# Two Strassen pairs in the output projection, and the third head's attention by float32r parts

## The chip, the core and the metric

The kernel runs on one core of a Trainium2 chip. The core has five engines that run side by side and wait for each other by semaphores: TensorE (PE, matmuls into the PSUM accumulators), VectorE (DVE), ScalarE (ACT), GpSimd (POOL) and SyncE (SP, which issues transfers; ACT issues some too). The metric is the device time of one execution in microseconds (us).

## The reference

One decoder layer on 512 tokens of width 1024, all in float32. It is the chain below; the middle line of the output projection and the two lines of the head are what the change touches.

```python
u    = rms_norm(x, mix_pre_g) * (1 + sc1) + sh1      # sh1, sc1, g1, sh2, sc2, g2 = split(silu(c) @ ada_w + ada_b)
qk_raw, v, o_pre, gates, glu = split(u @ w_in)
q, k = split(silu(causal_dwconv(qk_raw, 4 taps)))    # four heads of 256
# per head, chunks of 128 tokens:
scores = einsum("bhtd,bhsd->bhts", q, k) * exp(dmat - m)
num    = w_inter * (q @ C) + einsum("bhts,bhse->bhte", scores, v)
h    = rms_norm(num / den, ml_norm_g) * sigmoid(o_pre)
y    = silu(layer_norm(causal_dwconv(a * sigmoid(gt), 31 taps)))
mix  = concatenate([h, y]) @ w_out                   # 512 x 2048 times 2048 x 1024
x    = x + g1 * rms_norm(mix, mix_post_g)
f    = ConvFFN(rms_norm(x, ffn_pre_g) * (1 + sc2) + sh2)
x    = x + g2 * rms_norm(f, ffn_post_g)
```

## The kernel before

Most products of two float32 matrices are done in three float32r matmuls (`mm3`, L186). Each operand is split into a high part, a float32r copy that ACT makes, and a low part, the difference; the products high x high, high x low and low x high are accumulated. For weights `w_split` (L164) lets ACT make the high copy and POOL the low part; for activations `pair` (L451) lets DVE make the low part. Names end in h and l for the parts: `wo_0h`, `hl`, `yh`.

**Heads.** The loop over h does the attention of head h (`attention`, L500) while `head_proj` projects q, k and the output gate of head h + 1; `make_v` projects its values. `attention` is a generator whose steps are interleaved with the projections. Scores `s` of one key chunk go through DVE into `E` (the decay weights), and `o` is the product of E and v. `SPLIT` names the heads whose scores and values are done by parts; it is the fourth alone (`SPLIT = (H - 1,)`). The other heads use plain float32 matmuls (L514, L533). ACT copies o into `hn`, POOL works out its norm `fac`, DVE scales hn, PE turns it (`hT`), and DVE and ACT make the gated rows `hh`, `hl`. The taps of q and k (`conv4`) are three shifted multiply-adds on DVE into `q_0c`, `q_1c`, `k_2c`, `k_3c`, read from the projection's PSUM bank `qko`, and then a Silu on ACT.

**Output projection.** The 2048 rows of w_out are 16 blocks of 128: 0 to 7 belong to the heads (two each), 8 to 15 to the convolution. `MIX` gives their order. The left half of the columns is accumulated in the four banks `mixa`, one for 128 tokens, over all 16 blocks (`mix_first`, 12 matmuls of 512 columns for each block), while the attention of the fourth head is done in between. The right half, `mixb`, is done for the first 8 blocks block by block, and for the last 8 token tile by token tile (`mix_last`), because the norm and the feed-forward of the first tile start as soon as it is finished.

**Conditioning.** `mod`, 48 columns, is silu(c) times ada_w, done on DVE in 48 blocks (`ada_block`, L147): a load of 512 KB on ACT's queue and one 128 x 1024 multiply-accumulate with the output `junk`. Blocks 16 to 23 stand behind the convolution's last tap, 24 to 39 behind the fourth head's last low part (`last_lo`); `spare` is memory that the projection's input u leaves free. The gains made from them are turned by PE (`gT`) and sent through memory to become rows (`g1r`, `gs2r`, `sh2r`).

A scheduler sets the order on each engine from dependences and priorities. `in_order()` (L70) pins what is written inside it to the written order on DVE, ACT and POOL.

Of the kernel before, what the change touches and what calls it, by code (L numbers as in the profile page):

```python
# [22 lines left out]
H = 4  # L23
# [25 lines left out]
MIX = [*range(6), *range(8, 14), 6, 7, 14, 15]  # L49
# [3 lines left out]
def decoder_layer(ctx, tc, w_glu0, x, xT, c, adaT, vecs, w_glu, w_qko, w_v0, w_v, w_out, w_up, w_down, out):  # L53
# [93 lines left out]
    def ada_block(i, behind):  # L147

        if i % 6 < 4 and 24 <= i < 40:
            r = spare[0][:, 2 * (i % 6) : 2 * (i % 6) + 2, :].rearrange("p j t -> p (j t)")  # L150
        else:
            r = adas.tile([P, D], F32, tag="ada", name=f"ada_{i}")
        nc.scalar.dma_start(r, adaT[i // 2][:, (i % 2) * D : (i % 2 + 1) * D])
        junk = small.tile([P, D], BF16, tag="junk", bufs=1, name=f"junk_{i}")
        t = V.scalar_tensor_tensor(out=junk, in0=r, scalar=1.0, in1=cb, op0=ALU.mult, op1=ALU.mult, accum_out=mod[:, i : i + 1])  # L155
        tc.add_manual_dep(t.ins, behind.ins.name, mybir.DependencyInfo(mybir.DependencyClass.NoSync, mybir.DependencyReason.DATA),
                          reason="order on VectorE")
# [6 lines left out]
    def w_split(src, name, pool=None, tag="w", eng=None):  # L164
# [6 lines left out]
        (eng or G).tensor_tensor(out=lo[:, :n], in0=src, in1=hi[:, :n].bitcast(F32), op=ALU.subtract)  # L171
        return hi, lo

    def w_load(view, name, pool=None, tag="w"):

        n = view.shape[1]
        r = raws.tile([P, 2048], F32, tag="raw", name=name)
        nc.sync.dma_start(r[:, :n], view)
        return [w_split(r[:, a : min(a + T, n)], f"{name}_{a}", pool, tag) for a in range(0, n, T)]
# [6 lines left out]
    def mm3(ps, a, b, start, stop):  # L186

        PE.matmul(ps, a[0], b[0], start=start, stop=False)  # L188
        PE.matmul(ps, a[0], b[1], start=False, stop=False)  # L189
        PE.matmul(ps, a[1], b[0], start=False, stop=stop)  # L190
# [221 lines left out]
    SPLIT = (H - 1,)  # L412
# [38 lines left out]
    def pair(z, hi, lo):  # L451
        S.activation(hi, z, AF.Copy)
        V.tensor_tensor(out=lo, in0=z, in1=hi.bitcast(F32), op=ALU.subtract)
        return hi, lo

    def conv4(ps, i, name):
# [6 lines left out]
        S.activation(t, t, AF.Silu)  # L463
# [7 lines left out]
    last_conv4 = [None]  # L471
# [9 lines left out]
    def head_proj(h, i):  # L481
# [9 lines left out]
        else:  # L491
            t = slot(f"so{h}_{i}")
            S.activation(t, ps, AF.Tanh, scale=0.5)
            so.append(t)
        if (h, i) in CV_BEHIND:
            cv_block(CV_BEHIND[h, i], last_conv4[0])

    last_lo = [None]

    def attention(h):  # L500
# [46 lines left out]
        for tt in range(NT):  # L547
            hv = hn[tt // 2][:, (tt % 2) * DH : (tt % 2 + 1) * DH]
            V.tensor_scalar(out=hv, in0=hv, scalar1=fac[:, tt : tt + 1], scalar2=None, op0=ALU.mult)
        yield  # L550
        for e in range(2):
# [4 lines left out]
            t = so[e]  # L556
            V.scalar_tensor_tensor(out=t, in0=t, scalar=1.0, in1=tp, op0=ALU.add, op1=ALU.mult)
            hi, lo = slot(f"hh{h}_{e}", F32R), slot(f"hl{h}_{e}", F32R)
            g = ghalf[:, 2 * h + e : 2 * h + e + 1]
            S.activation(hi, t, AF.Copy, scale=g)  # L560
            last_lo[0] = V.scalar_tensor_tensor(out=lo, in0=t, scalar=g, in1=hi.bitcast(F32), op0=ALU.mult, op1=ALU.subtract)
            hy[2 * h + e] = (hi, lo)
# [87 lines left out]
    def send_rows(a, n, queue=nc.scalar):  # L650

        ps = mmbank(f"gT{a}") if a == KT else atbank(f"gT{a}")
        PE.transpose(ps[:n, :P], gains[:, a : a + n], ident)
        t = slot(f"gTs{a}")[:, :P]
        V.tensor_copy(t[:n, :], ps[:n, :P])
        for i in range(n // KT):
# [34 lines left out]
    KA = 8  # L691
# [4 lines left out]
    def wo_rows(hf, g):  # L696
        return w_load(w_out[hf, g], f"wo{hf}_{g}")
# [74 lines left out]
    def norm_rows():  # L772
        yb = rms_bcast(yr[0], T, 1.0 / D, "ry", cvbank)
        for j in range(KT):
            V.tensor_tensor(out=ys[j], in0=ys[j], in1=yb, op=ALU.mult)
            S.activation(ys[j], ys[j], AF.Silu, bias=vcol("cv_ln_b", j), scale=vcol("cv_ln_g", j))
            hi, lo = slot(f"yh{j}", F32R), slot(f"yl{j}", F32R)
# [4 lines left out]
    for h in range(H - 1):  # L782
# [50 lines left out]
    next(steps)  # L833
    for n in range(7, 10):
        mix_first(n)
    for _ in steps:
        pass
    spare.append(upool.tile([P, KT, T], F32, tag="ul", name="spare"))
    for i in range(24, 40):
        ada_block(i, last_lo[0])  # L840
    ada_done(24, 40)
    for n in range(10, 2 * KT):
        mix_first(n)
        if n == 10:
            send_rows(0, KT)
    mg = [slot(f"mg{tt}") for tt in range(NT)]
    x1 = [[slot(f"x1_{tt}_{hf}") for hf in range(2)] for tt in range(NT)]
    wide1 = vpool.tile([P, 2 * T + 8], F32, tag="vh", name="g1r")
    g1r = row(0, lambda n: [wide1[:, :T], wide1[:, T : 2 * T]], "g1")
    for tt in range(NT):  # L850
        for hf in range(2):
            nc.scalar.dma_start(x1[tt][hf], x[tok(tt), hf * T : (hf + 1) * T])
    for tt, ps in enumerate(mixa):
        V.tensor_tensor(out=mg[tt], in0=ps, in1=g1r[0], op=ALU.mult)
        sq_sum(ps, msq[:, 2 * tt : 2 * tt + 1], f"mixa{tt}")
    banks = [atbank(f"mixb{tt}") if tt < 2 else cvbank(f"mixb{tt}") for tt in range(NT)]
    for n_, k in enumerate(MIX[:KA]):
        if n_ % 4 == 0:
            wo = wo_rows(1, n_ // 4)
        for tt, ps in enumerate(banks):  # L860
            mm3(ps, (hy[k][0][:, tok(tt)], hy[k][1][:, tok(tt)]), wo[n_ % 4], n_ == 0, False)
    V.scalar_tensor_tensor(out=gains[:, KT : 2 * KT], in0=sc2[:, :, 0], scalar=1.0, in1=vcols("ffn_pre_g", 0, KT), op0=ALU.add, op1=ALU.mult)
    V.tensor_scalar(out=gains[:, KT : 2 * KT], in0=gains[:, KT : 2 * KT], scalar1=RD, scalar2=None, op0=ALU.mult)
    V.tensor_copy(gains[:, 2 * KT : 3 * KT], sc2[:, :, 1])
    wo = [w for g in range(KA // 4, 4) for w in wo_rows(1, g)]

    HT = T // 2
# [69 lines left out]
    up_w = {0: w_load(w_up[0], "wup0", slots, "t")}  # L937
    raw1 = raw_up(1)
    send_rows(KT, 2 * KT, nc.sync)
    gs2r = row(1, cvtile, "gs2", nc.sync)  # L940
    sh2r = row(2, cvtile, "sh2", nc.sync)
    raw2 = raw_up(2)
    early += [[mmbank(f"up{i}_{half}") for half in range(2)] for i in range(2)]
    with in_order():
        for tt in range(3):
            mix_last(tt, 0, 2 * KT - KA)
        up_split(1, raw1, slots, "t")
        r = chain_sums(0)
# [11 lines left out]
        mix_last(3, 7, 2 * KT - KA)  # L960
# [310 lines left out]
def _layout(i):  # L1271
# [9 lines left out]
    def tiles(w, starts, per):  # L1281
# [21 lines left out]
    wo = f("w_out")[0]  # L1303
    return {
# [10 lines left out]
        "w_out": c_(wo.reshape(2 * KT, P, 2, T)[MIX].reshape(4, NT, P, 2, T).transpose(3, 0, 2, 1, 4).reshape(2, 4, P, 4 * T)),  # L1315
# [22 lines left out]
```

## Time and profile before

| | |
|---|---|
| runs | 774.28, 771.67, 771.31 us (median 771.67) |
| profiled execution | 773.07 us, span 771.4 us, granted clock 0.997 |
| busy in the span | PE 758.4, DVE 610.1, ACT 403.8, POOL 352.2 us |
| third head's attention | about 261 to 300 us of the span |
| output projection, left half | from 320.4 us |
| gT8 turned | 392.7 us |

Times in the trace are us from the span's start. A row of the timeline gives start, duration, engine, line, operation, output and inputs (buffer numbers left out), shape, and how many instructions were merged in it; a bracket at its end is the idle time of the engine before it and what ended it. Neighbouring matmuls overlap, so their cost is taken from start to start. A row of the groups gives the busy time and, behind the comma, the mean in ns of one.

### The profile page before, as it was taken

Reading aid. Unit: us, or ns where it says so; the run is one execution under the profiler, and the core shown is the slowest. Engines: PE = TensorE matmul, PEld = TensorE weight load, DVE = VectorE, ACT = ScalarE, POOL = GpSimd, SP = SyncE. Lnnn points to the kernel's source line nnn. Section 1 sums busy time; section 2 is a strip of 40 time slices with the busy share of each in tenths; the row PEclk is TensorE's granted clock in tenths of the full one; section 3 lists DMA queues with packets and bytes.
Section 4 is the critical chain, followed back from the end, with each engine's and each line's share of the span. In section 5 each row is a group of like instructions: output and inputs, shape, how many; then the busy total and the mean of one; then the engine's idle time right before and its main releaser. Section 6 shows DMA issues by size and latency. Waiting matters only on the chain.

```text
span 771.4 us, 10631 instructions
## 1 busy us (share of the span) xinstructions
PE 758.4 (98%) x3709; PEld 637.5 (83%) x3709; DVE 610.1 (79%) x967; ACT 403.8 (52%) x761; POOL 352.2 (46%) x286
## 2 busy tenths in 40 slices
PE   7999999999999999999999999999999999999996
PEld 5788898778888888988888998888888888888885
DVE  6997999999999966756768798666556687799995
ACT  5447266776666447582253555444444444455762
POOL 2029578696798645443661456444444440000001
PEclk9999999999999999999999999999999999999998
DMA  8983214214022452434953753332233321777872
GB/s 320 377 301 132 90 55 164 82 40 151 30 84 107 153 179 105 164 110 164 366 199 126 253 197 130 130 130 88 110 117 129 130 89 62 255 271 241 298 260 109
DMA packets 36409, 125.33 MB, mean 162 GB/s; under 512 B 4194, under 2 KB 5634, under 8 KB 30468
## 3 DMA queue, kind: packets, MB, share of 16 engines
q1 hardware_dynamic: 24372, 96.17, 35.5%
q10 hardware_dynamic: 11984, 28.48, 10.6%
q8 instruction: 29, 0.48, 0.3%
q14 instruction: 24, 0.20, 0.1%
HBM read 113.22 MB, written 11.42 MB: 162 GB/s over the span
## 4 chain that ended last, share of the span: by engine, by line
PE 72%; DVE 21%; DMA 2%; ACT 2%; issue 2%; POOL 0%; ACTq 0%; DVEq 0%; POOLq 0%
PE up L189 10%; PE up L188 10%; DVE cv L731 10%; PE up L190 10%; PE p L1185 4%; PE glu L189 3%; PE glu L190 3%; PE glu L188 3%; PE p L189 3%; PE p L188 3%; PE p L190 3%; PE mixa L188 2%; PE mixa L190 2%; PE mixa L189 2%; PE mixb L189 2%; PE mixb L188 2%
## 5 line engine op out<-in xcount | busy, mean ns | idle before, releaser
L731 DVE SCALAR_TENSOR_TENSOR cv<-gt,cvw,cv 128x505 f32<-128x505 f32 (+24 forms) x200 | 137.3, 729 | 2.3 <-ACT cv L719 1.1
L685 POOL TENSOR_TENSOR ro2r<-ro2t,mhalf 128x1 f32<-128x1 f32 x1 | 0.5, 537 | 119.8 <-DVE ro2t L683 119.8
L727 POOL TENSOR_TENSOR cs<-cs,cs 128x510 f32<-128x510 f32 (+3 forms) x32 | 41.9, 1308 | 0.3
L171 POOL TENSOR_TENSOR wup_1024l<-wup,wup_1024h 128x512 fp32r<-128x512 f32 x20 | 27.4, 1372 | 31.6 <-ACT wup_1024h L170 31.6
L171 POOL TENSOR_TENSOR wup_0l<-wup,wup_0h 128x512 fp32r<-128x512 f32 x20 | 27.7, 1387 | 30.0 <-ACT wup_0h L170 30.0
L171 POOL TENSOR_TENSOR wup_1536l<-wup,wup_1536h 128x512 fp32r<-128x512 f32 x20 | 28.0, 1399 | 27.6 <-ACT wup_1536h L170 25.1
L155 DVE SCALAR_TENSOR_TENSOR junk<-ada,cb 128x1024 bf16<-128x1024 f32 x20 | 31.3, 1565 | 8.5 <-DMA ada<-in_adaT 8.4
L189 PE MATMUL up<-u2l,wup_0h 128*128 128x512 f32 (+1 forms) x100 | 36.5, 365 | 0.2 <-DVE u2l L910 0.2
L188 PE MATMUL up<-u2h,wup_0h 128*128 128x512 f32 (+1 forms) x100 | 36.5, 365 | 0.0
L188 PE MATMUL up<-u2h,wup_1024h 128*128 128x512 f32 (+1 forms) x100 | 36.4, 364 | 0.0
L190 PE MATMUL up<-u2h,wup_0l 128*128 128x512 f32 (+1 forms) x100 | 36.4, 364 | 0.0
L188 PE MATMUL up<-u2h,wup_512h 128*128 128x512 f32 (+1 forms) x100 | 36.4, 364 | 0.0
L189 PE MATMUL up<-u2l,wup_512h 128*128 128x512 f32 (+1 forms) x100 | 36.4, 364 | 0.0
L190 PE MATMUL up<-u2h,wup_512l 128*128 128x512 f32 (+1 forms) x100 | 36.4, 364 | 0.0
L188 PE MATMUL up<-u2h,wup_1536h 128*128 128x512 f32 (+1 forms) x100 | 36.4, 364 | 0.0
L189 PE MATMUL up<-u2l,wup_1536h 128*128 128x512 f32 (+1 forms) x100 | 36.4, 364 | 0.0
L190 PE MATMUL up<-u2h,wup_1536l 128*128 128x512 f32 (+1 forms) x100 | 36.4, 364 | 0.0
L190 PE MATMUL up<-u2h,wup_1024l 128*128 128x512 f32 (+1 forms) x100 | 36.4, 364 | 0.0
L189 PE MATMUL up<-u2l,wup_1024h 128*128 128x512 f32 (+1 forms) x100 | 36.3, 363 | 0.0
L171 POOL TENSOR_TENSOR wup_512l<-wup,wup_512h 128x512 fp32r<-128x512 f32 x20 | 27.7, 1383 | 14.0 <-ACT wup_512h L170 14.0
L725 ACT ACTIVATE cs<-gt,cvw 128x511 f32<-128x511 f32 (+4 forms) x40 | 27.4, 716 | 6.5 <-POOL cs L727 3.2
L170 ACT ACTIVATE wup_1024h<-wup 128x512 fp32r<-128x512 f32 x22 | 13.9, 631 | 25.1 <-PE up L189 20.4
(1072 smaller groups left out, 2667.0 us busy)
## 6 DMA issues: line engine op xcount, KB each, us to landing
wup<-in_w_up SPq DMA_DIRECT2D x22, 1024.0 KB, 6.5
wqko<-in_w_qko SPq DMA_DIRECT2D x12, 1024.0 KB, 4.8
ada<-in_adaT ACTq DMA_DIRECT2D x20, 512.0 KB, 4.6
ada<-in_adaT SPq DMA_DIRECT2D x16, 512.0 KB, 6.9
wo<-in_w_out SPq DMA_DIRECT2D x8, 1024.0 KB, 4.8
spare<-in_adaT ACTq DMA_DIRECT2D x12, 512.0 KB, 7.4
wd<-in_w_down SPq DMA_DIRECT2D x6, 768.0 KB, 6.7
g2kept<-g2d SPq DMA_DIRECT2D x11, 384.0 KB, 7.3
```

The source lines that it names most:

```text
L155: t = V.scalar_tensor_tensor(out=junk, in0=r, scalar=1.0, in1=cb, op0=ALU.mult, op1=ALU.mult, accum_out=mod[:, i : i + 1])
L170: S.activation(hi[:, :n], src, AF.Copy)
L171: (eng or G).tensor_tensor(out=lo[:, :n], in0=src, in1=hi[:, :n].bitcast(F32), op=ALU.subtract)
L188: PE.matmul(ps, a[0], b[0], start=start, stop=False)
L189: PE.matmul(ps, a[0], b[1], start=False, stop=False)
L190: PE.matmul(ps, a[1], b[0], start=False, stop=stop)
L685: G.tensor_tensor(out=r, in0=t, in1=mhalf[:, :1], op=ALU.pow)
L725: S.activation(t[:, d:], cvx[j][:, : T - d], AF.Copy, scale=w(CK - 1 - d))
L727: G.tensor_tensor(out=side[:, d:], in0=side[:, d:], in1=t[:, d:], op=ALU.add)
L731: last_tap[0] = V.scalar_tensor_tensor(out=cp[:, d:], in0=cvx[j][:, : T - d], scalar=w(CK - 1 - d), in1=cp[:, d:], op0=ALU.mult, op1=ALU.add)
L1185: PE.matmul(ps[q], x, y, start=False, stop=m == NM - 1 and i == 2, skip_group_check=True)
```

## The change

**Strassen pairs.** Conv blocks 12 to 15 leave `MIX`, which has 12 blocks now, and become `PAIRS` (12, 13) and (14, 15). For each pair, the two halves of the tokens, the two blocks of rows and the two halves of the columns make a product of 2 x 2 blocks, done with seven products (Winograd's form) in place of eight. One product (`block`) is two pairs x two token tiles x three parts = 12 matmuls of 512 columns. The order p1, p5, row blocks 10 and 11 of mixa, p2, p6, p4, p7, p3 is written out in one `in_order()` section. The sums of tokens (`token_sums`), of weight rows (`row_sums`, `row_last`, `ot1`), the low parts of both (`token_part`, `row_part`) and the additions between PSUM banks are on DVE; ACT makes the high parts and copies the intermediate products out (`op1`, `op5`, `ou`, `op7`). The raw weight rows (`w_os`, two loads of 1 MB into `wraw`) use memory that u leaves free. The additions are done in place: p5 and p3 in the banks mixb 0 and 1, p1, p6 and p7 in mixb 2 and 3, p2 in mixa 0 and 1, p4 in mixa 2 and 3. After the products mixb gets 4 blocks block by block (`KA = 4`, before 8) and 8 in `mix_last`.

**Third head.** `SPLIT` is now `(H - 2, H - 1)`.

**What moves with it.** Ada blocks 24 to 28 go into the third head's attention, behind taps of the fourth head's q and k; 29 to 34 ahead of hn of the fourth head; 35 to 39 into the written order. The row of g1 and the loads of x go from ACT's queue to SP's. The fourth head's gates (`gate`) are split off so that they can stand in the written order. gT8, `gs2r` and `sh2r` stand inside `mix_last(0)`, behind 5 of its 8 blocks. `wo1_8` and `wup0` are loaded into wraw.

```diff
-MIX = [*range(6), *range(8, 14), 6, 7, 14, 15]
+MIX = [*range(6), *range(8, 12), 6, 7]
+PAIRS = [(12, 13), (14, 15)]
...
-    SPLIT = (H - 1,)
+    SPLIT = (H - 2, H - 1)
...
-    KA = 8
+    HT = T // 2
+    KF = 12
+    KA = 4
...
+    def token_sums(za, zb, name):
+        sums, s4 = cvtile(f"os{name}"), cvtile(f"o4{name}")
+        s1, s2 = sums[:, :HT], sums[:, HT:]
+        V.tensor_tensor(out=s1, in0=za[:, HT:], in1=zb[:, HT:], op=ALU.add)
+        V.tensor_tensor(out=za[:, HT:], in0=za[:, :HT], in1=za[:, HT:], op=ALU.subtract)
+        V.tensor_tensor(out=s2, in0=s1, in1=za[:, :HT], op=ALU.subtract)
+        V.tensor_tensor(out=s4[:, :HT], in0=zb[:, :HT], in1=s2, op=ALU.subtract)
...
+    def row_part(which, m):
+        b = {"p1": 1, "p2": 0, "p6": 1, "p7": 2, "p3": 3, "p4": 0}.get(which)
+        z = ot1[m] if which == "p5" else wraw[m][:, b * T : (b + 1) * T]
+        wf[which, m] = w_split(z, f"o{which}_{m}", eng=V)
...
+    def block(which, m):
+        ps = {"p1": banks[2:], "p6": banks[2:], "p7": banks[2:], "p5": banks[:2], "p3": banks[:2], "p2": mixa[:2], "p4": mixa[2:]}[which]
+        for q in range(2):
+            mm3(ps[q], tf[m][which][q], wf[which, m], m == 0 and which in ("p1", "p5"), m == 1, True)
...
         if h == H - 2:
             norm_mean()
+            tc.cur_priority += LATER
+            for i in range(16, 24):
+                ada_block(i, last_tap[0])
+            for i in range(24, 29):
+                ada_block(i, taps[H - 1, 1 if i < 27 else 3], acts[H - 1, 0 if i < 27 else 2])
+            tc.cur_priority -= LATER
...
+    for m, r in enumerate(wraw):
+        nc.sync.dma_start(r, w_os[m])
...
+    mid = wo_rows(0, 8, 10)
...
+    for i in range(29, 35):
+        ada_block(i, last_pair[0], acts[H - 1, 5])
+    zb = token_sums(ys[6], ys[7], "1")
+    with in_order():
...
+        for q in range(2):
+            V.tensor_tensor(out=banks[q], in0=banks[q], in1=ou[q], op=ALU.add)
+        for m in range(2):
+            block("p3", m)
...
+        for q in range(2):
+            V.tensor_tensor(out=banks[2 + q], in0=banks[2 + q], in1=op5[q], op=ALU.add)
...
+        for i in range(37, 40):
+            ada_op(i, last_lo[0])
...
-        for tt in range(3):
-            mix_last(tt, 0, 2 * KT - KA)
+        mix_last(0, 0, 5)
+        send_rows(KT, 2 * KT, nc.sync)
...
+        mix_last(0, 5, KF - KA)
+        for tt in range(1, 3):
+            mix_last(tt, 0, KF - KA)
```

On PE, at the third head's scores (s is the scores of one key chunk, qkh and qkl the parts of q and k), before:

```order
L188 MATMUL v_3_2545<-wv_5h,uh 128x256
L189 MATMUL v_3_2545<-wv_5l,uh 128x256
L190 MATMUL v_3_2545<-wv_5h,ul 128x256
L514 MATMUL s_0_2720<-q_0c,k_2c 128x512
L514 MATMUL s_0_2720<-q_1c,k_3c 128x512
L514 MATMUL s_1_2724<-q_0c,k_2c 128x384
L514 MATMUL s_1_2724<-q_1c,k_3c 128x384
L188 MATMUL qko_0_2728<-uh,wqko_0_0h 128x512
```

and now:

```order
L211 MATMUL s_0_2748<-qkh_2479,qkh_2487 128x512
L211 MATMUL s_0_2748<-qkl_2480,qkh_2487 128x512
L211 MATMUL s_0_2748<-qkh_2479,qkl_2488 128x512
L211 MATMUL s_0_2748<-qkh_2483,qkh_2491 128x512
L211 MATMUL s_0_2748<-qkl_2484,qkh_2491 128x512
L211 MATMUL s_0_2748<-qkh_2483,qkl_2492 128x512
L211 MATMUL s_1_2758<-qkh_2479,qkh_2487 128x384
L211 MATMUL s_1_2758<-qkl_2480,qkh_2487 128x384
L211 MATMUL s_1_2758<-qkh_2479,qkl_2488 128x384
L211 MATMUL s_1_2758<-qkh_2483,qkh_2491 128x384
L211 MATMUL s_1_2758<-qkl_2484,qkh_2491 128x384
L211 MATMUL s_1_2758<-qkh_2483,qkl_2492 128x384
```

Four plain matmuls have become twelve, three for each, between the same neighbours.

On DVE, at the taps of the fourth head's q and k, before:

```order
L462 SCALAR_TENSOR_TENSOR q_1c<-qko_1_2767,vec,q_1c 128x511
L462 SCALAR_TENSOR_TENSOR q_1c<-qko_1_2767,vec,q_1c 128x510
L462 SCALAR_TENSOR_TENSOR q_1c<-qko_1_2767,vec,q_1c 128x509
L462 SCALAR_TENSOR_TENSOR k_2c<-qko_2_2798,vec,k_2c 128x511
L462 SCALAR_TENSOR_TENSOR k_2c<-qko_2_2798,vec,k_2c 128x510
L462 SCALAR_TENSOR_TENSOR k_2c<-qko_2_2798,vec,k_2c 128x509
```

and now:

```order
L487 SCALAR_TENSOR_TENSOR q_1c<-qko_1_2819,vec,q_1c 128x511
L487 SCALAR_TENSOR_TENSOR q_1c<-qko_1_2819,vec,q_1c 128x510
L487 SCALAR_TENSOR_TENSOR q_1c<-qko_1_2819,vec,q_1c 128x509
L174 SCALAR_TENSOR_TENSOR junk_3107,mod<-ada_3105,cb 128x1024
L174 SCALAR_TENSOR_TENSOR junk_3111,mod<-ada_3109,cb 128x1024
L487 SCALAR_TENSOR_TENSOR k_2c<-qko_2_2850,vec,k_2c 128x511
L174 SCALAR_TENSOR_TENSOR junk_3115,mod<-ada_3113,cb 128x1024
L487 SCALAR_TENSOR_TENSOR k_2c<-qko_2_2850,vec,k_2c 128x510
```

Three ada blocks (24 to 26) stand between the taps of q_1c and of k_2c; 27 and 28 follow those of k_3c.

On DVE, at the end of the seven products; the bank mixb 2 is `mixb_3725`, mixb 3 `mixb_3726`. Before, in this place stand the fourth head's gates and then ada blocks:

```order
L557 SCALAR_TENSOR_TENSOR so_5_2971<-so_5_2971,hT_1_3542 128x512
L561 SCALAR_TENSOR_TENSOR hl_0_3539<-so_4_2910,ghalf,hh_0_3538 128x512
L561 SCALAR_TENSOR_TENSOR hl_1_3549<-so_5_2971,ghalf,hh_1_3548 128x512
L155 SCALAR_TENSOR_TENSOR junk_3554,mod<-spare,cb 128x1024
L655 COPY gTs_3620<-gT_3618 8x128
L155 SCALAR_TENSOR_TENSOR junk_3557,mod<-spare,cb 128x1024
```

and now (op_0l and op_1l are the low parts of the rows for p3):

```order
L190 TENSOR_TENSOR op_0l<-wo_raw,op_0h 128x512
L190 TENSOR_TENSOR op_1l<-wo_raw,op_1h 128x512
L1003 TENSOR_TENSOR mixb_3723<-mixb_3723,ou 128x512
L1003 TENSOR_TENSOR mixb_3724<-mixb_3724,ou 128x512
L1008 TENSOR_TENSOR mixa_1372<-mixa_1372,op_0_3782 128x512
L1008 TENSOR_TENSOR mixa_1373<-mixa_1373,op_1_3783 128x512
L190 TENSOR_TENSOR wo_0l<-wo_0_3874,wo_0h 128x512
L190 TENSOR_TENSOR wo_1l<-wo_0_3874,wo_1h 128x512
L174 SCALAR_TENSOR_TENSOR junk_3919,mod<-spare,cb 128x1024
L1015 TENSOR_TENSOR mixb_3725<-mixb_3725,op_0_3784 128x512
L1015 TENSOR_TENSOR mixb_3726<-mixb_3726,op_1_3785 128x512
```

The additions into the right half's last two banks stand behind two additions each for mixb and mixa, two weight lows and ada block 36.

More of the change, by code (lines that the diff above doesn't have):

```diff
@@ L850, in decoder_layer @@
     for tt in range(NT):
         for hf in range(2):
[L852 to L861, printed above, removed]
```

267 lines of the change are left out of this document (195 added, 72 removed).

## The prediction

> **What bounds the kernel now.** I read the page first, then the busy time of each engine by stretches, then the timeline of TensorE (PE) and VectorE (DVE) around the two places that the change touches. From the page, in order: the span, the busy time, and the chain that ended last.
>
> ```profile
> span 771.4 us, 10631 instructions
> PE 758.4 (98%) x3709; PEld 637.5 (83%) x3709; DVE 610.1 (79%) x967; ACT 403.8 (52%) x761; POOL 352.2 (46%) x286
> PE 72%; DVE 21%; DMA 2%; ACT 2%; issue 2%; POOL 0%; ACTq 0%; DVEq 0%; POOLq 0%
> ```
>
> The stretches of the third head (250 to 290) and of the output projection (330 to 390); the columns are the busy time of PE, weight loads, DVE, ScalarE (ACT), GpSimd (POOL), then the granted clock, the DMA share and GB/s.
>
> ```profile
> 250.00:270.00 20.00, 19.67 (x126) 17.00 (x125) 18.29 (x22) 8.73 (x20) 12.19 (x8) 1.00 0.46 147
> 270.00:290.00 20.00, 19.55 (x89) 16.06 (x88) 12.12 (x20) 9.81 (x21) 8.73 (x6) 1.00 0.54 178
> 330.00:350.00 20.00, 20.00 (x104) 17.12 (x103) 9.24 (x14) 14.03 (x34) 10.50 (x10) 1.00 0.31 105
> 350.00:370.00 20.00, 20.00 (x94) 16.55 (x93) 13.92 (x22) 3.27 (x6) 4.37 (x4) 1.00 0.64 232
> 370.00:390.00 20.00, 20.00 (x90) 16.53 (x90) 15.93 (x22) 8.04 (x16) 16.90 (x10) 1.00 0.86 321
> ```
>
> In both stages PE sets the end: it is never idle from 330 to 390 and lacks 0.33 and 0.45 us in the two stretches of the third head. So time saved on PE is saved in the span, as long as DVE, ACT and the transfers still arrive in time. In the projection DVE has room (9 to 16 of 20 us), and the change spends that room.
>
> **Term 1, the Strassen pairs.** PE in the output projection and in the fourth head's values:
>
> ```profile
> 336.33 0.28 PE L529 MATMUL o<-v,Eh 128*128 128x258 f32 x1
> 337.41 0.40 PE L188 MATMUL mixa<-wo_512h,hh 128*128 128x512 f32 x1
> 340.13 0.28 PE L529 MATMUL o<-v,Eh 128*128 128x258 f32 x1
> 343.93 0.28 PE L529 MATMUL o<-v,Eh 128*128 128x258 f32 x1
> 345.36 0.40 PE L188 MATMUL mixa<-wo_1536h,yh 128*128 128x512 f32 x1
> ```
>
> One row block on the four token tiles is 12 matmuls, from 337.41 to 340.13: 2.72 us, 0.227 each (the 0.40 of a row is its busy time, and neighbours overlap). Two pairs of blocks cost 4 x 12 x 2 column halves = 96 matmuls before. Now they are seven products of 12, so 84. Twelve fewer: **-2.72 us**. The added matmuls are none; sums, lows and additions into PSUM go to DVE, copies to ACT.
>
> **Term 2, the third head by parts.** The same shapes stand in the trace both ways: plain fp32 in the second and third head, parts in the fourth.
>
> ```profile
> 215.25 0.59 PE L514 MATMUL s<-q_0c,k_2c 128*128 128x256 f32 x2
> 216.79 0.40 PE L189 MATMUL qko<-ul,wqko_1024h 128*128 128x512 f32 x1
> 261.34 1.12 PE L514 MATMUL s<-q_0c,k_2c 128*128 128x512 f32 x2 [0.33 <-DVE so L557]
> 264.68 0.39 PE L189 MATMUL qko<-ul,wqko_0h 128*128 128x512 f32 x1
> 282.86 1.47 PE L533 MATMUL o<-v,E 128*128 128x258 f32 x6
> 284.40 0.40 PE L189 MATMUL qko<-ul,wqko_1024h 128*128 128x512 f32 x1
> 296.39 1.90 PE L533 MATMUL o<-v,E 128*128 128x258 f32 x8
> 298.37 0.40 PE L189 MATMUL qko<-ul,wqko_1024h 128*128 128x512 f32 x1
> 317.88 0.48 PE L188 MATMUL s<-qkh,qkh 128*128 128x512 f32 x1
> 320.40 0.39 PE L188 MATMUL mixa<-wo_0h,hh 128*128 128x512 f32 x1
> 323.17 0.28 PE L188 MATMUL s<-qkh,qkh 128*128 128x256 f32 x1
> 324.50 0.77 PE L203 MATMUL ry_b<-ident,ry_r 128*128 128x128 f32 x5
> ```
>
> Each second row of the plain ones is the second projection matmul behind the group, so 0.227 is taken off. First score group (512 and 384 columns): 264.68 - 261.34 - 0.227 = 3.11 plain, 320.40 - 317.88 = 2.52 by parts, of which some 0.1 is the slow first matmul after a change of kind: -0.6 to -0.7. Second group (256 and 128 columns): 216.79 - 215.25 - 0.227 = 1.31 against 324.50 - 323.17 = 1.33: nothing. Values: 284.40 - 282.86 - 0.227 = 1.31 against 337.41 - 336.33 = 1.08, twice (the next group is as large), and 298.37 - 296.39 - 0.227 = 1.75 against 345.36 - 343.93 = 1.43: -0.78. Together **-1.45 us**. [...]
>
> **What is added elsewhere, and its cover.** DVE prices:
>
> ```profile
> 325.64 4.87 DVE L775 TENSOR_TENSOR gt<-gt,ry_b 128x512 f32<-128x512 f32 x8
> L779 DVE TENSOR_TENSOR yl<-gt,yh 128x512 fp32r<-128x512 f32 x8 | 7.5, 972 | 3.1 <-ACT yh L778 2.9
> L155 DVE SCALAR_TENSOR_TENSOR junk<-spare,cb 128x1024 bf16<-128x1024 f32 x12 | 18.1, 1505 | 4.8 <-DMA spare<-in_adaT 4.5
> L775 DVE TENSOR_TENSOR gt<-gt,ry_b 128x512 f32<-128x512 f32 x8 | 4.9, 680 | 0.0
> 348.01 1.14 DVE L549 TENSOR_SCALAR hn<-hn,fac 128x256 f32<-128x256 f32 x4 [2.04 <-POOL fac L546]
> 357.03 1.22 DVE L155 SCALAR_TENSOR_TENSOR junk<-spare,cb 128x1024 bf16<-128x1024 f32 x1
> 386.18 2.19 DVE L155 SCALAR_TENSOR_TENSOR junk<-spare,cb 128x1024 bf16<-128x1024 f32 x1
> 388.41 1.15 DVE L160 TENSOR_TENSOR mod<-mod,vec 128x16 f32<-128x16 f32 x1
> 390.84 1.23 DVE L863 TENSOR_SCALAR gains<-gains 128x8 f32<-128x8 f32 x1
> ```
>
> A 512-wide operation is 0.61 back to back (4.87/8) where it runs alone, and 0.97 in a stretch where POOL works beside it; an ada block (one 128x1024 multiply-accumulate) is 1.22 alone and up to 2.19.
>
> Third head: four score lows, four value lows and E's lows are some 6 us more on DVE between 240 and 275, and five ada blocks (24 to 28) come in behind the taps of the fourth head, 6 to 7.5 us into a stretch where DVE idles 7.9 of 20. They wait for loads that ACT issues only after q_0c's Silu, and behind them on DVE stand the taps (three shifted multiply-adds each) of k_2c and k_3c.
>
> ```profile
> 287.30 2.32 DVE L462 SCALAR_TENSOR_TENSOR k_2c<-qko,vec,k_2c 128x511 f32<-128x511 f32 x3 [1.95 <-ACT k_2c L460]
> 304.31 0.68 PE L188 MATMUL v<-wv_0h,uh 128*128 128x256 f32 x1
> ```
>
> PE needs the bank of k_2c again only for the values projection at 304.31, 14.7 us after the taps' old end, so I cost this wait at nothing. E no longer waits behind three ada blocks, so the 0.45 us go; the 0.33 before the scores may stay.
>
> Seven products: all times below are on the old clock, with the third head's saving left out. Three row blocks of 2.72 and eight transposes (some 0.9) follow 345.36, so the products run from 354.4, 2.72 each, with two row blocks between p5 and p2: p6 ends at 370.8, p7 at 376.2, p3 at 379.0. DVE has 40 operations from the end of hn to the last addition of op5 into the banks of the right half: 37 of 0.61, one half-wide and two ada blocks, 22.6 + 0.3 + 2.5 = 25.4 us. hn begins at 348.01 now; with six ada blocks put ahead of it I take its end as 350.2, and the last two additions, which also wait for ACT's copies of p7, end at about 378.1. PE asks for these banks after p3 and six matmuls, at 380.3: **about 2 us of slack**, the tightest place. The lows of each single product come some 3 to 4 us ahead. Cost taken: 0.
>
> Transfers: the two 1 MB loads of the Strassen rows wait until u is free (near 317), and the 0.5 MB of rows 8 and 9 stand behind them on SP's queue, while ACT's queue loads 2 MB of ada.
>
> ```profile
> GB/s 121 233 220 246 116 26 331 131 351 0 0 33 380 7 0 7 0 0 3 144 372 329 397 23 26 311 82 0 0 200 220 0 7 0 56 388 290 296 407 414
> wo<-in_w_out SPq DMA_DIRECT2D x7, 1024.0 KB, 4.8
> 326.65 1.52 ACT L776 ACTIVATE gt<-gt,vec 128x512 f32<-128x512 f32 x2
> ```
>
> In 2.5 us slices of 270 to 370, four from 317.5 on show 144, 372, 329 and 397 GB/s with both queues at work. At about 366, 4.5 MB take 12.9 us and rows 8 and 9 land near 331. ACT reaches its copy of them after five Silu and two copies, 326.65 + 4.7 = 331.4; behind it stand the copies that free the banks of o, with 2 us to spare. Cost 0; at the other end, 1 MB per 4.8 us, they land at 338.6 and PE waits 5.2. The x and g1 rows move to SP's queue behind weights that were asked for before; some 4 MB from 370 on land near 383 at the same pace, well ahead of x's use behind the last accumulation. gT8, now inside that accumulation, waits for the square sum of mixa0 behind mg0, which stands on DVE behind four more wide operations, ada 37 to 39 and the gains: 378.1 + 2.4 + 3.7 + 0.7 + 1.3 = 386.2 at the low prices, 392.2 with 2.19 for an ada block and the rows of 1.15 to 1.23 for the gains. PE wants it 63 matmuls after p3, at 379.0 + 14.3 = 393.3: cost 0, at the other end 1 if DVE comes late by 2 us.
>
> **The sum.** -2.72 - 1.45 = -4.17 us; the 0.45 us that go and about 0.4 of new short waits cancel. The profiled execution took 773.07 us (span 771.4 and 1.67 around it), so it would take 768.9; it stands 1.40 above the median of the three runs, 771.67, and on that basis the forecast is **767.5 us**.
>
> **Rivals.** *Short waits eat the gain.* The late rows 8 and 9 (to 5.2), gT8 (to 1), hn held behind six ada blocks at 2.19 (about 1): with 1 to 5 us of it the time is 768.5 to 772.5, within 0.5%. For it: PE had no slack to begin with and four queues are re-ordered; against it: each place has a reserve by the rows. Chance 0.36. [...]
>
> *DVE becomes the bound (slower).* Place: between hn and the additions into the right half's banks. If its 37 wide operations cost 0.97, as the eight lows beside POOL did, DVE is 37 x 0.36 = 13.3 us later; less the 2.2 of slack and some 0.5 in which DVE waits for ACT's copies anyway, PE waits 10.6: 767.5 + 10.6 = 778.1. It passes 0.5% slower (775.5) from 0.90 each on. Against it: POOL's lows of this stage move to DVE, so from about 350 to 379 POOL has nothing to run beside it. Chance 0.10.
>
> *The parts give nothing.* If in the third head they hold to the narrow shapes' price, only -2.72 stays: 769.0. Against it stand the fourth head's rows. Chance 0.04.
>
> **Numbers.** Forecast 0.50. About 0.5%, 3.9 us, is what a measurement of this kernel can tell from no change; the bound is at 767.8, close above my figure, so I put 0.47 of the forecast's chance on faster and 0.03 within. Faster 0.47, within 0.5% 0.43 (0.03 + 0.36 + 0.04), slower 0.10. Range: at the low end the 0.4 of new waits do not come, the other 0.33 of idle time in the third head goes too, and the run lies as far below its median as the lowest run shown (0.36): 767.5 - 0.4 - 0.33 - 0.36, about 766.4. The high end takes in short waits up to 6 us: 773.5. That leaves out about 0.04 below and 0.14 above.
>
> **What would show it.** Right: twelve matmuls of a product in 2.72 us without gaps, third-head scores in 2.5 and values in 1.08 and 1.43, DVE's op5 additions done before PE's use of the bank. Wrong: PE waiting for DVE's lows or additions, for o behind ACT's copy of rows 8, or for mixa0's square sum at gT8; or DVE operations over 0.7 us with POOL idle.

## The result, and the profile after

The changed kernel takes 774.14 us (median of 20 runs), the kernel before 772.70 us beside it: ratio 1.0023, 95% interval 1.0014 to 1.0032. It is slower by 0.23%, less than the 0.5% of the text above but clear of zero. The forecast was 767.5 us with a range up to 773.5, so the time lies 0.6 us above the range. Of the 6.64 us between forecast and time, 1.03 are the basis: the forecast started from 771.67 us for the kernel before, which took 772.70 here. The profiled execution took 773.82 us against 773.07 before. Of the kernels below, one execution of e7 took 3752 us, about five times the others, and is left out of its comparison.

From the page of the changed kernel: span, busy time, chain.

```profile
span 772.1 us, 10715 instructions
PE 755.0 (98%) x3715; PEld 635.8 (82%) x3715; DVE 645.1 (84%) x1027; ACT 415.5 (54%) x787; POOL 334.4 (43%) x272
PE 64%; DVE 27%; ACT 3%; issue 3%; DMA 2%; POOL 1%; ACTq 1%; DVEq 0%; POOLq 0%
```

PE did less work (755.0 against 758.4) and the span did not follow: on the chain DVE's share went from 21% to 27%. The stretches say where (columns as in the prediction):

```profile
250.00:270.00 20.00, 18.50 (x124) 16.72 (x122) 19.86 (x27) 8.32 (x19) 11.84 (x7) 1.00 0.36 118
270.00:290.00 20.00, 19.07 (x93) 15.88 (x93) 14.83 (x25) 8.72 (x15) 7.05 (x6) 1.00 0.56 179
330.00:350.00 20.00, 20.00 (x105) 17.01 (x104) 19.06 (x35) 14.33 (x36) 3.34 (x3) 1.00 0.41 141
350.00:370.00 20.00, 20.00 (x94) 16.64 (x93) 17.78 (x33) 10.99 (x21) 2.62 (x3) 1.00 0.51 187
370.00:390.00 20.00, 20.00 (x90) 16.57 (x89) 19.93 (x27) 11.66 (x22) 8.57 (x5) 1.00 0.74 275
```

In the Strassen stretches (330 to 390) PE is never idle, though DVE is nearly full. In the third head DVE is busy 19.86 of 20 us (18.29 before, in the row from 250), and PE loses 1.50 and 0.93 us. The four new waits, in PE's timeline (the first two in the third head, the third behind it, the last in `mix_last`):

```profile
269.99 0.39 PE L211 MATMUL s<-qkh,qkh 128*128 128x256 f32 x1 [1.47 <-DVE E L542]
291.22 0.39 PE L556 MATMUL o<-v,Eh 128*128 128x258 f32 x1 [2.15 <-ACT hn L564]
321.83 0.44 PE L211 MATMUL s<-qkh,qkh 128*128 128x384 f32 x1 [1.11 <-DVE ry_t L230]
396.78 0.28 PE L691 MATMUL gT<-ident,gains 128*16 128x128 f32 x1 [0.67 <-ACT mixa0junk L719]
```

Three landmarks on PE split the span: the first score of the third head, the first matmul of mixa, and the first transpose of the feed-forward's input (`xT`).

| us | before | after | forecast |
|---|---|---|---|
| first score to first mixa (third-head stage) | 59.06 | 62.67 | 57.61 |
| first mixa to xT (projection stage) | 88.78 | 86.85 | 86.06 |
| everything else | 623.56 | 622.58 | 623.56 |

The forecast column takes only the two terms off. The rest differs by 0.98 before and after, 0.69 of it in the first 40 us. By the second head's scores, up to which PE does the same work in all these kernels, their profiled executions stand up to 2.3 us apart; so kernels are compared below by their two stages as well.

**How two waits come about.** DVE's rows in the third head:

```profile
259.58 0.68 DVE L591 SCALAR_TENSOR_TENSOR so<-so,hT 128x512 f32<-128x512 f32 x1
...
261.11 2.26 DVE L174 SCALAR_TENSOR_TENSOR junk<-ada,cb 128x1024 bf16<-128x1024 f32 x1
...
263.30 1.77 DVE L583 SCALAR_TENSOR_TENSOR hl<-so,ghalf,hh 128x512 fp32r<-128x512 f32 x1
265.00 2.31 DVE L174 SCALAR_TENSOR_TENSOR junk<-ada,cb 128x1024 bf16<-128x1024 f32 x1
...
269.26 1.14 DVE L542 SCALAR_TENSOR_TENSOR E<-s,E 128x512 f32<-128x512 f32 x2
...
271.46 1.77 DVE L474 TENSOR_TENSOR El<-E,Eh 128x512 fp32r<-128x512 f32 x1
273.15 2.31 DVE L174 SCALAR_TENSOR_TENSOR junk<-ada,cb 128x1024 bf16<-128x1024 f32 x1
...
280.55 1.23 DVE L174 SCALAR_TENSOR_TENSOR junk<-ada,cb 128x1024 bf16<-128x1024 f32 x1 [1.95 <-DMA ada<-in_adaT]
...
282.64 0.74 DVE L487 SCALAR_TENSOR_TENSOR q_0c<-qko,vec,q_0c 128x509 f32<-128x509 f32 x1
```

ACT's, after:

```profile
283.46 1.28 ACT L488 ACT_TABLE_LOAD   x1 [4.32 <-DVE gains L708]
...
290.08 0.76 ACT L485 ACTIVATE k_2c<-qko,vec 128x512 f32<-128x512 f32 x1
...
290.79 0.38 ACT L564 ACTIVATE hn<-o 128x256 f32<-128x256 f32 x1
```

The same places before, first DVE's, then one each of ACT and PE:

```profile
260.61 1.27 DVE L557 SCALAR_TENSOR_TENSOR so<-so,hT 128x512 f32<-128x512 f32 x2
261.80 1.21 DVE L155 SCALAR_TENSOR_TENSOR junk<-ada,cb 128x1024 bf16<-128x1024 f32 x1
...
268.56 0.68 DVE L515 SCALAR_TENSOR_TENSOR E<-s,E 128x512 f32<-128x512 f32 x1
...
278.28 1.52 DVE L462 SCALAR_TENSOR_TENSOR q_0c<-qko,vec,q_0c 128x510 f32<-128x510 f32 x2
287.21 0.38 ACT L537 ACTIVATE hn<-o 128x256 f32<-128x256 f32 x1
289.62 1.47 PE L533 MATMUL o<-v,E 128*128 128x258 f32 x6
```

The wait at E: E's first multiply starts 9.68 us after the first of the `so` operations, 7.95 before. Two value lows (0.67 together, start to start) and an ada block of 2.26 in place of 1.21 stand ahead of it.

The wait at hn: the last tap of q_0c ends at 283.38 instead of 279.80, 3.58 us later: lows of E, ada blocks and a late load stand ahead of it. The Silu of q_0c waits for it on ACT (the bracket names the small operation on the gains that ended last; before, it names q_0c itself, with the Silu's table load again 0.08 us behind the last tap), and the copies of o into hn stand behind: the first ends at 291.17 instead of 287.59. Before, PE came for that bank 2.03 us after the copy; it now comes 0.55 earlier. 3.58 + 0.55 - 2.03 = 2.10, nearly the 2.15 of the wait. The wait is put down to ACT, but its cause is VectorE's queue ten microseconds earlier.

The first low of E, at 271.46, costs 1.77 us; the 512-wide lows of the Strassen rows (`op`), with no GpSimd row beside them, took 0.68 or 0.69 each. GpSimd works on weight lows in the stretch of E, and one of its rows covers the first 1.22 us of that low.

```profile
271.25 1.43 POOL L190 TENSOR_TENSOR wqko_1024l<-wqko,wqko_1024h 128x512 fp32r<-128x512 f32 x1 [1.13 <-ACT wqko_1024h L189]
```

The ada blocks from 250 to 400 with no GpSimd row beside them took 1.21 to 1.23 us, those with one 1.21 to 2.31. So a row beside GpSimd's work can be longer and need not be; what makes up the 1.77 - 0.68 = 1.09 us is not shown by any run here.

### The profile page after: what moved, and what is told of

Its sections match the earlier page's. It is cut to its first block, busy times and chain, and to the rows that moved or that the text cites. A ratio compares the mean times of both kernels' runs of the same rounds, so it can differ in the third digit from the quotient of the medians.

```text
span 772.1 us, 10715 instructions
## 1 busy us (share of the span) xinstructions
PE 755.0 (98%) x3715; PEld 635.8 (82%) x3715; DVE 645.1 (84%) x1027; ACT 415.5 (54%) x787; POOL 334.4 (43%) x272
## 4 chain that ended last, share of the span: by engine, by line
PE 64%; DVE 27%; ACT 3%; issue 3%; DMA 2%; POOL 1%; ACTq 1%; DVEq 0%; POOLq 0%
PE up L211 31%; DVE cv L817 10%; PE glu L211 8%; PE p L211 8%; PE p L1356 4%; PE mixa L211 4%; PE mixb L211 3%; DVE junk L174 3%; PE glu L337 2%; PE v L211 1%; DVE k_3c L487 1%; DVE q_1c L487 1%; DVE ydl L831 1%; DVE k_2c L487 1%; DVE q_0c L487 1%
## 5 line engine op out<-in xcount | busy, mean ns | idle before, releaser
L174 DVE SCALAR_TENSOR_TENSOR junk<-ada,cb 128x1024 bf16<-128x1024 f32 x24 | 38.6, 1610 | 5.7 <-DMA ada<-in_adaT 5.5
L190 POOL TENSOR_TENSOR wup_0l<-wup,wup_0h 128x512 fp32r<-128x512 f32 x19 | 26.0, 1368 | 29.6 <-ACT wup_0h L189 29.6
```

The lines of the kernel that those rows point to most:

```text
L190: op = (eng or G).tensor_tensor(out=lo[:, :n], in0=src, in1=hi[:, :n].bitcast(F32), op=ALU.subtract)
```

## The experiments

Theory 1: VectorE has no room in the third head for the parts' lows (four each of q and k, v, and E: 2.9 + 1.7 + 3.0 us by their rows) on top of ada blocks 16 to 23, and the blocks 24 to 28 are too much in the fourth head's taps; the savings on PE are real. Rivals: the loads come late; or TensorE, 1.5 us faster, merely meets earlier what was late anyway. Later: the order alone fails, and VectorE had the room.

| kernel | median us | ratio to before, 95% | third-head stage | projection stage |
|---|---|---|---|---|
| changed | 774.14 | 1.0023 (1.0014 to 1.0032) | 62.67 | 86.85 |
| e1 Strassen only | 772.96 | 1.0014 (1.0003 to 1.0025) | 61.56 | 86.85 |
| e2 parts only | 775.19 | 1.0031 (1.0020 to 1.0042) | 62.55 | 89.66 |
| e3 blocks 16-23 short | 769.31 | 0.9963 (0.9949 to 0.9977) | 58.68 | 86.85 |
| e4 blocks 24-28 short | 774.08 | 1.0023 (1.0011 to 1.0034) | 62.66 | 86.85 |
| e5 one load for 16-23 | 775.21 | 1.0036 (1.0023 to 1.0048) | 63.23 | 86.85 |
| e6 Strassen, blocks respread | 771.01 | 0.9979 (0.9964 to 0.9994) | 58.94 | 86.78 |
| e7, e9 both, respread | 774.31 | 1.0029 (1.0012 to 1.0045) | 61.71 | 87.54 |
| e8 third head's lows gone | 770.43 | 0.9969 (0.9954 to 0.9985) | 59.51 | 86.87 |
| e10 e6 with block 28 moved | 770.08 | 0.9959 (0.9942 to 0.9976) | 60.06 | 86.04 |
| e11 both, E's lows on POOL | 773.86 | 1.0013 (1.0000 to 1.0026) | 60.87 | 86.04 |

The two stages are those of one profiled execution, which is not always a typical one: e10's took 772.43 us, the longest of its eight, and e11's 772.33, the second shortest of twelve. In the row of e7 and e9, one kernel, the time is e7's and the stages are e9's, whose one execution took 776.14.

**e1 and e2: each half alone.** e1 is the changed kernel, e2 the kernel before, with one line each:

```diff
 e1
-    SPLIT = (H - 2, H - 1)
+    SPLIT = (H - 1,)
 e2
-    SPLIT = (H - 1,)
+    SPLIT = (H - 2, H - 1)
```

> The changed kernel with the parts in the fourth head alone, as before; the Strassen pairs and every moved ada block stay. Stage meant below: from the third head's first score to the first matmul of mixa, 59.1 us before, 62.7 after. Theory 1 (the parts' lows overfill VectorE's queue in the third head): TensorE's three waits there (E 1.5, hn 2.2, ry_t 1.1) shrink to 0.5 or less each, the stage is 58.6 to 59.5 us, and the time is 1.5 to 2.5 us below before (twelve matmuls fewer, -2.7, and the wait at gT8, +0.8). Rival 2 (ada loads that land late hold VectorE): the hn wait stays, stage 60.5 to 61.5, time within 0.7 us of before. Rival 3 (ada blocks 24 to 28, now among the taps): hn and ry_t waits stay, stage above 61, time up to 1.5 us above before.

> The kernel before with the third head by parts and nothing else. Theory 1: TensorE waits for E and for hn in the third head as in the changed kernel, the stage of the third head (59.1 us before) is 59.5 to 62 us, and the time is 0.5 to 3 us above before. Rival 2: as the ada loads stand where they stood, the waits stay at 0.5, stage 57.2 to 57.8, time 1.2 to 2 us below before. Rival 3: the same as rival 2, since blocks 24 to 28 stand in the projection here.

PE's two longest waits in e2 but for the start-up's (total, times, longest):

```profile
PE o L529 <- ACT hn L537: 1.9, 1, 1.9
PE s L188 <- DVE E L515: 1.5, 1, 1.5
```

Neither half is a gain. The parts alone, with no ada block moved, bring the waits at hn and E with nearly the sizes of the changed kernel; so these belong to the lows and the blocks 16 to 23, not to 24 to 28. In e2 the gains' transpose waits as well (0.74), and the projection stage is 0.88 longer than before. In e1 the hn wait is gone and that for ry_t stays, with one for so before it and the transpose's, so its stage, 61.56, misses the 58.6 to 59.5 of theory 1; e4 and e6 put the waits for ry_t and so down to the blocks 24 to 28:

```profile
PE s L211 <- DVE ry_t L230: 1.1, 1, 1.1
PE ry_s L217 <- DVE so L591: 0.9, 1, 0.9
...
PE gT L691 <- ACT mixa0junk L719: 0.7, 1, 0.7
```

**e3 and e4: VectorE's time for the blocks taken away.** The multiply-adds are cut to 64 of 1024 columns, the loads stay (the sums of these blocks are incomplete).

```diff
+        w = 64 if 16 <= i < 24 else D       # e3;  e4: 24 <= i < 29
-        t = V.scalar_tensor_tensor(out=junk, in0=r, scalar=1.0, in1=cb, ...)
+        t = V.scalar_tensor_tensor(out=junk[:, :w], in0=r[:, :w], scalar=1.0, in1=cb[:, :w], ...)
```

> The changed kernel with the multiply-adds of ada blocks 16 to 23 cut to 64 of 1024 columns; their loads stay, the sums are left incomplete. Some 10 us of VectorE's work leave the third head. Theory 1: the E and hn waits (1.5 and 2.2) go, the stage is 57.0 to 58.0 us (62.7 after, 59.1 before), and the time is 3 to 4.5 us below the changed kernel. Rival 2: since the loads remain as late or nearly, the hn wait stays above 1 and the stage is above 60. Rival 3: only the E wait goes, stage 60.5 to 61.5.

> The changed kernel with the multiply-adds of ada blocks 24 to 28 cut to 64 of 1024 columns; their loads stay, the sums are left incomplete. Theory 1: the E and hn waits stay (they end before these blocks), the ry_t wait (1.1) goes, stage 61 to 62.7 us, time 0 to 1.5 us below the changed kernel. Rival 3: the hn wait goes too, stage 59 to 60.5. Rival 2: as theory 1.

In e3 the waits at E and hn are gone and the stage is 3.99 us shorter; the kernel, with less work, beats the one before. The ry_t wait stays (1.1), and the stage is 0.7 above the range expected. Its PE timeline shows the parts undisturbed:

```profile
259.76 0.40 PE L212 MATMUL s<-qkh,qkh 128*128 128x512 f32 x1
...
262.22 0.39 PE L212 MATMUL qko<-uh,wqko_0h 128*128 128x512 f32 x1
...
279.97 0.28 PE L557 MATMUL o<-v,Eh 128*128 128x258 f32 x1
...
281.05 0.39 PE L212 MATMUL qko<-uh,wqko_1024h 128*128 128x512 f32 x1
```

Scores 2.46 us (3.11 plain), values 1.08 (1.31 plain): the prediction's prices. In e4 these waits of the changed kernel remain, and the transpose's with 0.7:

```profile
PE o L557 <- ACT hn L565: 2.0, 1, 2.0
PE s L212 <- DVE E L543: 1.5, 1, 1.5
```

The one for ry_t is gone: it comes from blocks 24 to 28. That the stage is no shorter goes with the granted clock: it was 0.87 and 0.79 in e4's two stretches from 290 to 300 (1.00 in the changed kernel), and the 24 matmuls behind e4's wait at hn took 7.10 us in place of 5.46 (last section).

**e5: late loads?** Blocks 17 to 23 use the rows of block 16 and have no load (their sums are wrong).

```diff
+        if 17 <= i < 24:
+            ada_rows[i] = ada_rows[16]
+            return
```

> The changed kernel, where the ada blocks 17 to 23 have no load of their own and use the rows of block 16 (their sums are wrong; VectorE's work and its order stay). Theory 1 (VectorE has too much to do in the third head: seven ada blocks plus 7.6 us for the parts' lows): nearly nothing changes, E's wait stays at about 1.5 us and the wait at hn loses at most the last link, block 23's late landing (1.95 us of VectorE), so 0 to 1.9 us less, 772 to 774. Rival (the loads come late, VectorE had time): both waits go, about 3.5 us less, near 770.5, the third head's stage below 59.5 us.

The time did not fall. PE's wait at hn shrank from 2.15 to 1.57, so the late load was about 0.6 us of it; the wait at E went, but only because a block without a load now stands between the two `so` of the second head, and PE waits there:

```profile
263.42 0.44 PE L214 MATMUL s<-qkh,qkh 128*128 128x384 f32 x1 [0.81 <-DVE so L594]
...
290.60 0.39 PE L559 MATMUL o<-v,Eh 128*128 128x258 f32 x1 [1.57 <-ACT hn L567]
```

The scaling of hn on DVE comes 46.1 us after the first score in both kernels, and what PE gained it gave back there (waits for so, 1.03, and ry_t, 0.29). The stage is even 0.56 longer than in the changed kernel: the six 384-column matmuls ahead of mixa alone took 1.72 us in place of 1.15 (last section). So the loads are a link, not the cause; theory 1's number for the wait at E was wrong all the same.

**e8: the lows taken away.** The products of parts stay, with the high part in place of each low one in the third head (scores and values are rounded).

```diff
+        last_high = S.activation(hi, z, AF.Copy)
+        if third[0]:
+            return hi, hi
...
+                vl = [va[:, cc, :DH] for cc in range(NT)]
```

> The changed kernel without the twelve lows of the third head on VectorE: the products of parts read the rounded part a second time in place of the low (TensorE's work, ScalarE's rounded parts and the ada blocks stay; scores and values of that head are rounded). Theory 1 (the lows' 7.6 us on top of the blocks 16 to 23 are what VectorE has no room for): the waits at E and hn go as they did with short blocks 16 to 23, the third head's stage is about 58.7 us (62.67 in the changed kernel), the ry_t wait of about 1.1 may stay, the time about 770. Rival (TensorE, 1.5 us faster, only meets earlier what was late anyway): the hn wait stays at 1 to 2 us, the stage is above 60.5 and the time above 771.5.

```profile
PE s L211 <- DVE ry_t L230: 1.1, 1, 1.1
...
PE s L211 <- DVE E L547: 0.4, 1, 0.4
```

No wait at hn, and E's is what it was before the change. PE is as fast here as in the changed kernel (first scores 2.46 us against 2.56, nine matmuls of values 1.08 against 1.07), so the rival that it merely comes earlier falls. With e3 the cause of these two waits is shown from both sides: take away either the lows or the blocks, and they go.

**e6 and e10: one head, blocks in other gaps.** e6 is e1 with the blocks 24 to 28 moved and the gains' transpose after seven blocks; e10 moves block 28 once more.

```diff
 e6
-            for i in range(24, 29):
-                ada_block(i, taps[H - 1, 1 if i < 27 else 3], acts[H - 1, 0 if i < 27 else 2])
+            ada_block(24, taps[H - 1, 0])
+            ada_block(25, taps[H - 1, 0])
+            ada_block(26, taps[H - 1, 1], acts[H - 1, 0])
+            ada_block(27, taps[H - 1, 2], acts[H - 1, 1])
...
-    for i in range(29, 35):
+    for i in range(28, 35):
...
-        mix_last(0, 0, 5)
+        mix_last(0, 0, 7)
 e10 (on e6)
+            ada_block(28, taps[H - 1, 3], acts[H - 1, 1])
...
-    for i in range(28, 35):
+    for i in range(29, 35):
```

> The Strassen half alone (third head plain), with the ada blocks 24 to 28 put into other gaps: 24 and 25 behind the first taps of the fourth head, 26 behind the second, 27 behind the third, 28 with the blocks 29 to 34; and the transpose of the gains after seven of the eight blocks in place of five. Theory 1: the waits for ry_t (1.1 us and some 1.4 about it) and for the gains' transpose (0.7) go, the stage from the third head's first scores to the first projection matmul is about 59.1 us, as before the change, the projection 86.2, so some 3 us under the Strassen half alone as measured (772.96), near 769.5 and 0.35% under the kernel before. Rival (the short waits only move, since VectorE has too little room in the whole fourth head): 772 to 773, the ry_t wait at another place.

> As e6_one_head_respread, with block 28 taken out of the queue ahead of the Strassen sums and put behind the last taps of the fourth head, where VectorE waits 2.7 us for ScalarE. Theory 1: the gains' transpose no longer waits (0.6 us in e6, since VectorE came 1.2 us later there), the ry_t wait stays away, 0.5 us less than e6: about 770.5. Rival (one block there is one too many): the fourth head's so or ry_t wait is back with 0.5 to 1 us, 771 to 772.

Both beat both kernels, e10 by 0.41% (0.24 to 0.58%) against the one before. In e6 the ry_t wait is away and the stage is back at 58.94; the transpose still waits 0.6, since block 28 holds VectorE up ahead of the Strassen sums: the rows `mg` behind the gains start 73.61 us after the first matmul of mixa, 72.32 in e10. In e10 that wait is gone and ry_t is back with 0.8 (its expectation's rival; the time is theory 1's). There block 28 takes 1.22 us ahead of the fourth head's hn, and block 27 came later, as VectorE waited longer for its load (1.93 in e6):

```profile
294.08 2.35 DVE L174 SCALAR_TENSOR_TENSOR junk<-ada,cb 128x1024 bf16<-128x1024 f32 x1 [2.54 <-DMA ada<-in_adaT]
```

The intervals of the two overlap, so which is better stays open.

**e7, e9 and e11: both halves kept.** e7 and e9 are one kernel, with the blocks 16 to 28 spread by hand. e11 is e10 with the parts in the third head and its lows of E on GpSimd.

```diff
 e7, e9
+            for i, behind, asked in ((16, last_tap[0], None), (17, last_tap[0], None), (18, e1[0], None), (19, e1[0], None),
+                                     (20, e2[0], e2[1]), (21, t[0], e2[1]), (22, t[1], z[0]), (23, t[1], z[0]),
+                                     (24, t[2], z[1]), (25, t[3], z[1]), (26, t[2], z[0])):
...
+    ada_block(27, lows[H - 1, 1][0], lows[H - 1, 1][1])
+    ada_block(28, lows[H - 1, 3][0], lows[H - 1, 3][1])
 e11
+                E[h][cc] = pair(E[h][cc], *halves_e[cc], eng=G if h == H - 2 else V)
```

> Both halves of the change, with the ada blocks 16 to 28 spread over the third and fourth head (16, 17 behind the last tap of the third head; 18 to 21 behind E's lows; 22 to 26 behind the taps of the fourth head; 27 and 28 behind E's lows of the fourth head) and the transpose of the gains after seven of the eight blocks. Theory 1 (only the order on VectorE fails): the waits at E, hn and ry_t go, the third head's stage is about 57.3 to 58 us and the time near 768. Rival (VectorE has no room for the parts' lows at all between 240 and 330 us, in whatever order): the waits stay at 2 us or more together, 771 to 773.

> The same kernel as e7_both_respread, whose profiled execution took 3752 us with matmuls of 1.19 us and says nothing of the order. The timed runs gave 774.31, so theory 1 in its narrow form (only the order on VectorE fails) expects what it did not get. Now: if VectorE has no room in whatever order, waits of 2 us or more together stand before E, hn, so or ry_t, and VectorE is busy over 95% from 240 to 300 us; if it has, the waits are short and the time went to a slower granted clock.

> Both halves of the change, the third head's four lows of E on GpSimd in place of VectorE, the blocks 24 to 28 and the gains' transpose as in e10. Theory 1: VectorE is relieved of 3.3 us (its lows of E), less what GpSimd beside it costs; the wait at E stays near 1 us (it comes before these lows), that at hn shrinks from 2 to about 0.5, ry_t's is away: the stage about 59.5 us and the time 769.5 to 770.5. Rival (the four operations stand ahead of the weight lows on GpSimd's queue or slow VectorE by as much): TensorE waits for wqko's lows, or hn stays late, 772 to 774.

In e9 no wait stands at E or hn any more: PE comes to hT of the third head 49.98 us after the first score, 54.16 in the changed kernel. But the wait comes in the fourth head:

```profile
PE ry_s L217 <- DVE so L592: 1.6, 1, 1.6
...
PE hT L591 <- ACT E L645: 0.8, 1, 0.8
```

DVE has not come earlier by as much: hn is scaled 44.8 us after the first score (46.1), and on the way it waited 5.5 us for loads of ada blocks, most of it at two:

```profile
279.71 1.23 DVE L174 SCALAR_TENSOR_TENSOR junk<-ada,cb 128x1024 bf16<-128x1024 f32 x1 [2.08 <-DMA ada<-in_adaT]
...
287.47 1.63 DVE L174 SCALAR_TENSOR_TENSOR junk<-ada,cb 128x1024 bf16<-128x1024 f32 x1 [2.06 <-DMA ada<-in_adaT]
```

So the order could take the two waits out of the third head, but this order pushed the work and its loads into the next. VectorE is busy 33.60 of the 40 us from 260 to 300, so at most 89% from 240 to 300: not the 95% of "no room in whatever order", but the waits are not short either. Theory 1's "only the order fails" is not shown.

In e11 waits of 1.81 for hn and 1.47 for E are left, and the time is its rival's; ry_t's and the transpose's waits are gone. The lows' move did end q_0c's taps earlier, 20.59 us after the first score in place of 23.07. But block 25, in the place it has in e10, now stands inside the taps of q_1c, where ACT waits 4.06 us for them ahead of the copies into hn. So e11 does not say what the lows' move alone would bring, and whether some order lets the parts pay in the third head stays open.

## Why the prediction was wrong

- **Strassen, -2.72: right.** Where the transpose does not wait (e10, e11) the projection stage is 86.04, 2.74 less than before. VectorE's lows stood 0.60 apart at 0.68 each, as the eight in 4.87 us had said. The second row below starts 0.08 us before the first one ends. The additions of op5 were done 2.5 us ahead (2 in the text). From the timeline of the changed kernel:

```profile
372.59 0.68 DVE L190 TENSOR_TENSOR op_1l<-wo_raw,op_1h 128x512 fp32r<-128x512 f32 x1
373.19 0.68 DVE L190 TENSOR_TENSOR op_0l<-wo_raw,op_0h 128x512 fp32r<-128x512 f32 x1
...
379.14 1.38 DVE L1015 TENSOR_TENSOR mixb<-mixb,op 128x512 f32<-128x512 f32 x2
381.67 0.39 PE L211 MATMUL mixb<-wo_0h,hh 128*128 128x512 f32 x1
```

  The additions end at 380.52; PE reaches bank 2 six matmuls (1.36 us) after the last row. The rival that DVE becomes the bound there fell.
- **Parts, -1.45: right on PE.** Without new waits the third-head stage of the changed kernel would be 57.09 (below), 1.97 less than before, of which 0.45 is the old wait at E: -1.52.
- **The step that failed** is "Third head: four score lows, four value lows and E's lows are some 6 us more on DVE ..., so I cost this wait at nothing", with "E no longer waits behind three ada blocks, so the 0.45 us go". The work was 7.6 us, a quarter more than said. Its cover was the error. E itself stands behind two ada blocks and two value lows. Three of E's four lows stand not before 275 but between 275 and 283, ahead of q_0c's taps and among them. The text looked at the one bank of k_2c that PE needs at 304, and took room from a mean over 270 to 290; but q_0c's taps stand at 277 to 280, where VectorE had no idle time in the kernel before, and behind them on ACT stand, through the Silu, the copies that free the banks of o, with 2.03 us to spare. Start to start against undisturbed groups, the waits cost 1.75 us at E, 2.44 at hn and 1.39 at ry_t: 5.58 us in place of the "0.4 of new short waits". The first two go without the lows (e8), the third without blocks 24 to 28 (e4).
- **gT8**: the bound of up to 1 us was the right one to fear; it cost 0.8. VectorE's blocks 37 to 39 took 2.2 to 2.3 us each and the gains 1.2, the high prices of the text.
- **Short waits eat the gain** named the right kind of outcome, at places of which only gT8 paid; rows 8 and 9 and the hn of the fourth head cost nothing. It was 1.6 us too low at its top (772.5 against 774.14).

In the spans of the two profiled executions: -4.17 forecast, +5.06 in the third head, +0.79 in the projection, -0.98 elsewhere, together +0.70; the medians moved by +1.44.

## What to carry to other kernels

Look for the cover of added work at the place in the queue where it will stand, not in a busy share over twenty microseconds: the first operation that it delays, the engine that waits for that one, and everything queued behind it there. What PE, 98% busy, saves here also comes off the reserve of the other engines: it came 0.55 us earlier to the bank of hn, where the reserve had been 2.03. A transfer or block of work moved as filler is worth a second look even when the main edit is sound: moving five of them differently, and one transpose, turned the Strassen half from a loss of 0.14% into a gain of 0.4%.

## What the runs showed of the hardware

**Behind some waits the granted clock falls, at a price of up to 1.6 us.** In e2, PE's timeline around the wait at hn:

```profile
291.23 0.39 PE L529 MATMUL o<-v,Eh 128*128 128x258 f32 x1 [1.88 <-ACT hn L537]
...
293.40 0.63 PE L189 MATMUL qko<-ul,wqko_0h 128*128 128x512 f32 x1
293.83 0.63 PE L190 MATMUL qko<-uh,wqko_0l 128*128 128x512 f32 x1
```

and its stretch behind it:

```profile
290.00:295.00 5.00, 3.77 (x14) 3.38 (x15) 2.25 (x3) 4.59 (x16) 3.10 (x3) 0.67 0.46 157
```

The granted clock falls to 0.67 (1.00 in the five microseconds before), and 512-column matmuls stand 0.43 apart in place of 0.227; spacing of nearly twice the usual lasts from 291.69 to 295.10 us. The block of 24 behind it took 6.49 us in e2 and 7.10 in e4 (behind a wait of 1.96), and 5.46 in the changed kernel, whose own wait of 2.15 us brought no such fall; nor did the 1.81 of e11. e9 shows it after its waits of 0.8 and 1.6 us (0.89 and 0.77 in the two stretches from 315), and e5 after its wait of 1.03 us for so (512-column matmuls 0.43 apart, six of 384 columns in 1.72 us), but not after its 1.57 at hn. So the length of a single wait does not decide it in these runs: idle times of 1.03 to 1.96 us stand ahead of the falls in e2, e4, e5 and e9, and behind others of 1.57 to 2.15 there was none. No run here shows what else it takes.
